# A two-branch mixer layer on one core: the first branch gated and split per head pair, the first attention group's preparation recorded beside the last scan

## The chip, the cores and the metric

One Trainium2 chip, one of its cores. The metric is device time in microseconds for one execution of the whole program, as the median of several runs. The engines are TensorE (PE, its weight loads PEld), VectorE (DVE), ScalarE (ACT), GpSimd (POOL) and SyncE (SP, which here only issues DMA transfers).

## The reference

One layer of a hybrid model over 640 tokens (128 of context, 512 latent), width 1024:

```
h = rmsnorm(x) * (1 + scale) + shift                     # scale, shift, gate from the condition
za, ga, q, kb, vb, gb, ma, mb = split(h @ w_in)          # one wide projection
r, k, v, wd, ad = split(short_conv(za))
for d in (forward, backward):                            # RWKV-7 scan, 16 heads of 64
    s = s * w_t + (s @ -kk_t) (kk_t a_t) + v_t k_t ;  y_d = s @ r_t
y = groupnorm(y_fwd + y_bwd) * ln_w + ln_b + bonus
branch_a = (y * silu(ga)) @ w_oA
o = banded grouped-query attention(rope(q), rope(kb), vb) + cached context keys, with a sink
branch_b = (o * silu(gb)) @ w_oB
out = x + gate * ((sigmoid(ma) * branch_a + sigmoid(mb) * branch_b) @ w_out) ; rmsnorm
```

The outputs are the two normed token blocks, the context's new keys and values, and the final scan states.

## The kernel before

**Layout.** Channels lie on the 128 partitions, the 640 tokens along the free axis. Each large product is in float32r with split operands: x = hi + lo, w = hi + lo, and three matmuls (hi·hi, hi·lo, lo·hi) per 128-row block. One block of 128 output columns is 48 matmuls of 128x320 in two PSUM halves (tag `g`, two buffers). Weights are loaded raw (`wr`, three buffers of 256 KB), cast on ACT (`wh`) and subtracted on POOL (`wl`).

**First stage: scan and filler.** The 16 heads are eight pairs (`NPAIR`), pair 0 to pair 7. For each pair there are `front` (decays, keys), `back` and `invert` (the inverse of the chunk matrices), `items` (five sets of chunk products), `chain` (ten dependent steps of the scan: two over the context, eight over the latents) and `finish` (group norm, transposes to `yT`, the bonus `bv` added on POOL, store to `a_dram[i]`). The matmuls that don't depend on the scan, the projections of the pairs and the *filler* (44 blocks: `kb`, `vb`, `q`, `ga`, `gb`, `ma`, `mb`, each spilled to DRAM), fill PE between the steps. `deal` writes out this order: a model clock (`Clock`) advances with each recorded instruction, and after every six filler matmuls each stream (`chains`, `finishes`, `all_items`, `fronts`, `backs`, in that order of right of way) is stepped where its model time has come. PE, ACT, DVE and POOL execute this part in the recorded order. Each engine runs its instructions strictly in order; an instruction that waits holds up those behind it.

**Between the stages.** `gate_rows` (16 products with `wg`, 256 KB each, through the `wr` buffers) and all that follows are placed by the scheduler by priority: earlier code first, `tc.cur_priority` moves it. So some of it lands among the last instructions of the scan.

**Second stage: attention and branch A.** `v_side` transposes cached keys and values, `k_side(g)` and `q_side(g)` rotate (`rope`) and split keys and queries of group g (0 to 3), `attend(g)` computes the softmax and the products with the values. The first call of the generator `branch_a` loads the eight `a_dram[k]` as `lda`, gates them with `ga` and splits them into `ah` and `al` (DVE, ACT, DVE); each further call is one of its eight blocks of 48 matmuls. The list `NBA` says how many blocks stand behind each group, `GPREP` behind which group the preparation is recorded.

**Third stage.** `branch_b` (8 blocks of 48) and `output` (240 matmuls, final norm).

Names in the profile: `g<-hh,wh` is a filler matmul, `g<-wg` a gate row, `st<-U,XT`, `st<-SB`, `ur<-SB,S`, `st<-SB,S`, `ur<-St,ar` are the five groups of matmuls of a chain step, `mi<-ident 32x320` is the second stage of `invert`, `g<-ah` is branch A, `ur<-KH,qt` a score product, `nm` a row maximum, `den` the softmax's denominator. All instructions recorded through `Timed` have the line of that helper (L139).

Of the kernel before, what the change touches and what calls it, by code (L numbers as in the profile page):

```python
# [51 lines left out]
GPREP = 1  # L52
PPREP = -600
NBA = [0, 3, 3, 2]
# [116 lines left out]
def hybrid_step(ctx, tc, a):  # L171
# [323 lines left out]
    def spill(col, dst, kind):  # L495

        def ev(half, o, s):
            t = T([P, HALF], "stg", 2, name="stg")
            if kind == "plain":
                act.copy(out=t, in_=o)  # L500
            else:
                act.activation(out=t, in_=o, func=AF.Tanh, scale=0.5)

            def rest():
                if kind == "silu":
                    dve.scalar_tensor_tensor(out=t, in0=t, scalar=1.0, in1=o, op0=ALU.add, op1=ALU.mult)
                nc.sync.dma_start(out=dst[:, s], in_=t)
            return rest
        return gemm_block(w_in, col, hh, hl, ev)
# [26 lines left out]
    def filler():  # L536

        for nm, col, nb, kind in (("kb", COL_KB, 2, "plain"), ("vb", COL_VB, 2, "plain"), ("q", COL_Q, 8, "plain"),
                                  ("ga", COL_GA, 8, "silu"),
                                  ("gb", COL_GB, 8, "silu"), ("ma", COL_MA, 8, "tanh"), ("mb", COL_MB, 8, "tanh")):  # L540
            for b in range(nb):
                spills[nm, b] = dram_.tile([P, TOK], F32, name="sp_%s%d" % (nm, b))
                yield spill(col + P * b, spills[nm, b], kind)
# [35 lines left out]
    a_dram = [dram_.tile([P, TOK], F32, name=f"a_dram{i}") for i in range(8)]  # L579
# [588 lines left out]
    def rope(x, outs):  # L1168

        sh = T([P, LAT], "tmp", 3, name="sh")  # L1170
        dve.stream_shuffle(out=sh, in_=x, mask=[(p + 16) % 32 for p in range(32)])
        t1 = T([P, LAT], "tmp", 3, name="t1")
        pool_e.tensor_tensor(out=t1, in0=x, in1=cosT, op=ALU.mult)
        dve.tensor_tensor(out=sh, in0=sh, in1=sinT, op=ALU.mult)
        for rows, dst in outs:
            dve.tensor_tensor(out=dst, in0=t1[rows], in1=sh[rows], op=ALU.add)

    def v_side():
        ck = T([P, 4, CH], "S", 5, name="ck")
# [4 lines left out]
        pt = PSC()  # L1184
        for b in range(2):
            pe.transpose(out=pt[:, b * P:(b + 1) * P], in_=ck[:, 2 * b:2 * b + 2, :].rearrange("p g d -> p (g d)"),
                         identity=ident)
        act.copy(out=kp.rearrange("p b x -> p (b x)"), in_=pt[:, 0:2 * P])
        vt_ = [T([P, 256], "SB", 10, name="vtok") for _ in range(5)]
        for b in range(2):  # L1190
            vz = unspill("vb", b, "rkv", 3)
            for t0, nt in ((0, 4), (4, 1)):
                pt = PSC()
                for t in range(nt):
                    pe.transpose(out=pt[:, t * P:(t + 1) * P], in_=vz[:, (t0 + t) * P:(t0 + t + 1) * P], identity=ident)
                for t in range(nt):
                    act.copy(out=vt_[t0 + t][:, P * b:P * b + P], in_=pt[:, t * P:(t + 1) * P])
# [6 lines left out]
    def k_side(g, kp):  # L1204
# [9 lines left out]
        pt = PSC()  # L1214
        pe.transpose(out=pt[:, 0:CH], in_=R[0:64, 6 * P:], identity=ident[0:64, 0:64])
        if g % 2 == 0:
            kt.append(T([P, 2, CH], "lraw", 1, name="kt"))
        act.copy(out=kt[-1][:, g % 2, :], in_=pt[:, 0:CH])
        if g % 2:
            nc.sync.dma_start(out=a["new_k"][0, 0, g - 1:g + 1].rearrange("g t d -> t g d"), in_=kt[-1])  # L1220
        rope(R[:, P:P + LAT], [(slice(0, P), R[:, P:P + LAT])])
# [4 lines left out]
        act.copy(out=H, in_=R)  # L1226
        pool_e.tensor_tensor(out=L, in0=R, in1=H.bitcast(F32), op=ALU.subtract)
# [4 lines left out]
    def q_side(g):  # L1232

        Q = []
        for b in range(2):
            q = unspill("q", 2 * g + b, "rkv", 3)
            rope(q[:, CTX:TOK], [(slice(0, P), q[:, CTX:TOK])])
# [8 lines left out]
            for h in range(2):  # L1246
                hr, lr = slice(64 * h, 64 * h + 64), slice(64 - 64 * h, 128 - 64 * h)
                act.copy(out=qs[h][hr, :], in_=q[hr, :])
                dve.tensor_tensor(out=qs[h][lr, :], in0=q[hr, :], in1=qs[h][hr, :].bitcast(F32),
# [285 lines left out]

    with tc.tile_pool(name="psc", bufs=1, space=PSUM) as pools["scan"], tc.manual_schedule(engines=ORDERED):
        deal(products(plan()), [chains(), finishes(), all_items(), fronts(), backs()])
# [3 lines left out]
    cosT = T([P, LAT], "kk", 1, name="cosT")  # L1541
    sinT = T([P, LAT], "cs", 1, name="sinT")
    nc.scalar.dma_start(out=cosT, in_=a["c_cos"])
    nc.scalar.dma_start(out=sinT, in_=a["c_sin"])
# [10 lines left out]
    kp, vt_, cv = v_side()  # L1555
    ba = branch_a()
    nxt = k_side(0, kp), q_side(0)
    for g in range(4):
        (KH, KL), Q = nxt
        if g < 3:  # L1560
            nxt = k_side(g + 1, kp), q_side(g + 1)
# [66 lines left out]
```

## Time and profile before

| | us |
|---|---|
| median of 3 runs (range) | 1475.28 (1470.62 to 1478.62) |
| the profiled execution, its span | 1471.97, 1470.2 |
| PE busy, share of the span | 1307.1, 89% |
| DVE, ACT, POOL busy | 791.8, 677.0, 455.1 |
| mean granted TensorE clock | 0.941 |

Where times below are points, they are microseconds from the span's start. A clock of 1.00 is 2.4 GHz, 0.50 is 1.2 GHz.

### The profile page before, as it was taken

The numbers are of one execution on the slowest core, as the hardware profiler recorded it, in microseconds if no ns is written. First come the engines' busy times: TensorE is split into PE (matmuls) and PEld (weight loads), VectorE is DVE, ScalarE is ACT, GpSimd is POOL, SyncE is SP. The second block draws the span as 40 slices with busy tenths as digits, with TensorE's granted clock in tenths as the row PEclk, the third lists the DMA queues.
The fourth block names the chain that finished last, engine by engine and source line by source line (L and its number), as shares of the span: only waits on it lengthen the run. The fifth ranks groups of instructions, "written<-read, shape, count | busy, mean of one in ns | idle before, by whom it ended". The sixth has DMA issues, their size and how long they took to land.

```text
span 1470.2 us, 40278 instructions
## 1 busy us (share of the span) xinstructions
PE 1307.1 (89%) x16959; PEld 1079.7 (73%) x16959; DVE 791.8 (54%) x1818; ACT 677.0 (46%) x1661; POOL 455.1 (31%) x476
## 2 busy tenths in 40 slices
PE   5699999999989999998998999999852889999996
PEld 0499888888878878887887878887441456668975
DVE  2446724654663455475464246336218887763547
ACT  2435563464365346436534635633524456554222
POOL 0333343343233234333332323331214031324530
PEclk9699999999999999999999999999955699999999
DMA  9143322222221222222231231322412341225532
GB/s 324 40 125 116 122 63 82 83 68 85 87 75 58 88 65 89 82 80 82 82 92 57 80 93 57 91 88 85 128 54 82 103 125 50 87 69 179 164 108 94
DMA packets 154419, 139.05 MB, mean 95 GB/s; under 512 B 16435, under 2 KB 130294, under 8 KB 154238
## 3 DMA queue, kind: packets, MB, share of 16 engines
q1 hardware_dynamic: 144328, 126.27, 27.8%
q10 hardware_dynamic: 9910, 10.21, 2.1%
q8 instruction: 133, 2.18, 0.6%
q14 instruction: 48, 0.39, 0.1%
HBM read 102.88 MB, written 33.56 MB: 93 GB/s over the span
## 4 chain that ended last, share of the span: by engine, by line
PE 64%; DVE 12%; issue 7%; ACT 6%; DMA 4%; POOL 2%; SPq 0%; DVEq 0%; ACTq 0%; POOLq 0%
PE g L139 34%; PE mi L139 10%; PE st L139 8%; PE sc L139 7%; PE ur L139 5%; DMA wr<-in_w_oB 1%; DMA wo<-in_w_out 1%; POOL wl L139 1%; DVE St L139 1%; DVE ytok L139 1%; DVE X L139 1%; ACT SB L139 1%; DVE o L139 1%; POOL wol L139 1%; ACT L139 1%
## 5 line engine op out<-in xcount | busy, mean ns | idle before, releaser
L139 POOL TENSOR_TENSOR wl<-wr,wh 128x512 fp32r<-128x512 f32 x170 | 229.4, 1352 | 666.8 <-ACT wh L139 620.0
L139 PE MATMUL g<-hh,wh 128*128 128x320 f32 (+1 forms) x1104 | 376.4, 341 | 11.4 <-DVE stg L139 4.6
L139 PE MATMUL g<-hl,wh 128*128 128x320 f32 (+1 forms) x1104 | 346.6, 314 | 1.7 <-POOL hl L139 1.5
L139 PE MATMUL g<-hh,wl 128*128 128x320 f32 (+1 forms) x1104 | 346.4, 314 | 0.0
L139 PEld LDWEIGHTS g<-hh,wh 128*128 128x128 f32 x1104 | 211.4, 191 | 31.0 <-issue 6.5
L139 PEld LDWEIGHTS g<-hl,wh 128*128 128x128 f32 x1104 | 211.9, 192 | 3.2 <-POOL hl L139 2.5
L139 PEld LDWEIGHTS g<-hh,wl 128*128 128x128 f32 x1104 | 212.4, 192 | 2.4 <-issue 1.9
L139 ACT CAST wh<-wr 128x512 fp32r<-128x512 f32 x170 | 104.4, 619 | 15.5 <-DMA wr<-in_w_oB 7.8
L139 ACT COPY SB<-st 64x128 f32<-64x128 f32 x160 | 41.6, 260 | 146.1 <-PE st L139 145.2
L139 DVE SCALAR_TENSOR_TENSOR St<-St,pc,st 128x64 f32<-128x64 f32 x128 | 30.2, 277 | 121.8 <-PE st L139 98.8
L139 ACT COPY U<-st 128x128 f32<-128x128 f32 x80 | 21.2, 266 | 159.0 <-DVE St L139 141.2
L139 DVE SCALAR_TENSOR_TENSOR stg<-g,vt,stg 128x127 f32<-128x127 f32 (+1 forms) x144 | 60.8, 436 | 62.0 <-ACT stg L139 59.4
L139 PE MATMUL mi<-ar,bk 64*64 64x64 f32 (+1 forms) x960 | 71.8, 248 | 7.5 <-DVE XT L139 7.4
L139 DVE TENSOR_TENSOR U<-ur,U 128x128 f32<-128x128 f32 x72 | 20.8, 289 | 94.7 <-PE ur L139 79.7
L139 POOL TENSOR_TENSOR S<-S,smask 128x512 f32<-128x512 f32 x40 | 50.3, 1256 | 63.5 <-ACT S L139 63.5
L139 ACT COPY SB<-sc 64x256 f32<-64x256 f32 (+1 forms) x160 | 55.2, 372 | 31.2 <-PE sc L139 29.4
L139 PEld LDWEIGHTS mi<-ar,bk 64*64 64x64 f32 (+1 forms) x960 | 61.7, 157 | 9.2 <-issue 6.8
L139 DVE TENSOR_TENSOR S<-sc,smask 128x512 f32<-128x512 f32 x40 | 27.4, 685 | 61.4 <-PE mi L139 46.0
L139 ACT ACTIVATE Pl<-ur,nm 128x384 f32<-128x384 f32 (+1 forms) x64 | 40.6, 635 | 36.9 <-DVE nm L139 30.1
L139 PE MATMUL ur<-KH,qt 128*128 128x512 f32 (+2 forms) x80 | 35.1, 443 | 22.7 <-ACT Pc L139 10.1
L139 ACT COPY PT<-sc 128x512 f32<-128x512 f32 x60 | 35.1, 584 | 39.3 <-PE sc L139 37.7
L139 DVE TENSOR_REDUCE nm<-ur 128x1 f32<-128x384 f32 (+2 forms) x68 | 41.5, 623 | 19.5 <-PE ur L139 18.7
(284 smaller groups left out, 2916.5 us busy)
## 6 DMA issues: line engine op xcount, KB each, us to landing
wr<-in_w_in SPq DMA_DIRECT2D x138, 256.0 KB
sp_rkv<-stg SPq DMA_DIRECT2D x48, 160.0 KB
rkv<-sp_rkv SPq DMA_DIRECT2D x24, 320.0 KB
wa_t<-in_w_ada SPq DMA_DIRECT2D x11, 512.0 KB
wg<-in_w_ada SPq DMA_DIRECT2D x16, 256.0 KB
wr<-in_w_oA SPq DMA_DIRECT2D x16, 256.0 KB
wr<-in_w_oB SPq DMA_DIRECT2D x16, 256.0 KB
wo<-in_w_out SPq DMA_DIRECT2D x16, 256.0 KB
```

The lines of the kernel that those rows point to most:

```text
L139: return f(**kw)
```

## The change

1. `finish` does the gating: when the pair's block of `ga` has been spilled, it loads it, multiplies, splits into hi and lo, and stores both halves, so `a_dram[i]` is [128, 2, 640]. The filler begins with `ga` so that it is there. `branch_a`'s first call is now 16 loads straight into `ah` and `al`, and is recorded ahead of group 0 instead of behind group 1; `NBA` goes from [0, 3, 3, 2] to [2, 3, 2, 1].
2. `finishes` moves behind `chains`, `all_items`, `fronts` and `backs`.
3. `v_side`, `k_side(0)`, `q_side(0)` become generators and are dealt with the last scan as three more streams, last in right of way; groups 1 to 3 run them through at once (`whole`) as before. They use other buffers; the five value tiles become one, evacuated with one instruction per PSUM tile.

```diff
-GPREP = 1
 PPREP = -600
-NBA = [0, 3, 3, 2]
+NBA = [2, 3, 2, 1]
...
-        for nm, col, nb, kind in (("kb", COL_KB, 2, "plain"), ("vb", COL_VB, 2, "plain"), ("q", COL_Q, 8, "plain"),
-                                  ("ga", COL_GA, 8, "silu"),
-                                  ("gb", COL_GB, 8, "silu"), ("ma", COL_MA, 8, "tanh"), ("mb", COL_MB, 8, "tanh")):
+        for nm, col, nb, kind in (("ga", COL_GA, 8, "silu"), ("kb", COL_KB, 2, "plain"), ("vb", COL_VB, 2, "plain"),
+                                  ("q", COL_Q, 8, "plain"), ("gb", COL_GB, 8, "silu"), ("ma", COL_MA, 8, "tanh"), ("mb", COL_MB, 8, "tanh")):
...
         pool_e.tensor_tensor(out=yT, in0=yT, in1=bv, op=ALU.add)
-        nc.sync.dma_start(out=a_dram[i], in_=yT)
-        yield
+        yield lambda: done.get(("ga", i))
+        sg = T([P, TOK], "bv", 1, name="us_ga")
+        nc.sync.dma_start(out=sg, in_=spills["ga", i])
+        clock.run.ready = max(clock.run.ready, clock.at["pe"] + 5)
+        yield
+        dve.scalar_tensor_tensor(out=yT, in0=yT, scalar=0.5, in1=sg, op0=ALU.mult, op1=ALU.mult)
+        yield
+        hi = T([P, TOK], "bv", 1, F32R, name="ah")
+        act.copy(out=hi, in_=yT)
+        nc.sync.dma_start(out=a_dram[i][:, 0], in_=hi.bitcast(F32))
+        yield
+        dve.tensor_tensor(out=yT.bitcast(F32R), in0=yT, in1=hi.bitcast(F32), op=ALU.subtract)
+        nc.sync.dma_start(out=a_dram[i][:, 1], in_=yT)
+        yield
...
         for k in range(KB):
-            f = T([P, TOK], ("tmp", "ytok")[k % 2], 1, name="lda")
-            nc.sync.dma_start(out=f, in_=a_dram[k])
-            sg = unspill("ga", k, "rkv", 1)
-            dve.scalar_tensor_tensor(out=f, in0=f, scalar=0.5, in1=sg, op0=ALU.mult, op1=ALU.mult)
             hi = T([P, TOK], "h", 16, F32R, name="ah")
             lo = T([P, TOK], "h", 16, F32R, name="al")
-            act.copy(out=hi, in_=f)
-            dve.tensor_tensor(out=lo, in0=f, in1=hi.bitcast(F32), op=ALU.subtract)
+            nc.sync.dma_start(out=hi.bitcast(F32), in_=a_dram[k][:, 0])
+            nc.sync.dma_start(out=lo.bitcast(F32), in_=a_dram[k][:, 1])
...
+    def first_values():
+        last = us[NPAIR - 1]
+        yield lambda: last.get("itemized") and last.get("prepared")
+        first["v"] = yield from v_side()
+
+    def first_keys():
+        last = us[NPAIR - 1]
+        yield lambda: "q" in first and "kp" in first and last.get("prepared")
+        first["k"] = yield from k_side(0, first["kp"], ("DG", "E"))
+
+    def first_queries():
+        yield lambda: us[NPAIR - 1].get("ready") and us[NPAIR - 2].get("finished") and us[NPAIR - 1].get("itemized")
+        for tag, src in (("kk", "c_cos"), ("cs", "c_sin")):
+            trig.append(T([P, LAT], tag, 1, name=src))
+            nc.scalar.dma_start(out=trig[-1], in_=a[src])
+        first["q"] = None
+        first["q"] = yield from q_side(0, ("ytok", "rkv"))
...
-        deal(products(plan()), [chains(), finishes(), all_items(), fronts(), backs()])
+        deal(products(plan()), [chains(), all_items(), fronts(), backs(), finishes(), first_values(), first_queries(), first_keys()])
...
+    base = tc.cur_priority
+    tc.cur_priority = PPREP + base
+    next(ba, None)
+    tc.cur_priority = base
...
-        if g == GPREP:
-            tc.cur_priority = PPREP + base
-            next(ba, None)
-            tc.cur_priority = 2000000 + base
```

What the order of instructions becomes, at three places.

**PE at the end of the filler.** Before, the last filler matmuls are followed by the last two of pair 6's ten chain steps:

```order
L139 MATMUL g<-hh,wl 128x320
L139 MATMUL g<-hl,wh 128x320
L139 MATMUL st<-U,XT 64x64 x4
L139 MATMUL g<-wg,csil 2x512
L139 MATMUL st<-SB 64x64 x4
```

Now the last of pair 6's steps starts 42 filler matmuls ahead of this place, and pair 7's `invert` follows at once:

```order
L138 MATMUL g<-hh,wl 128x320
L138 MATMUL g<-hl,wh 128x320
L138 MATMUL mi<-ident 32x320 x4
L138 MATMUL mi<-X,DG 32x32 x40
L138 MATMUL mi<-ident 32x320 x4
```

The two steps moved ahead of the filler's end; of the 16 `wg` products three instead of seven stand between the filler's end and pair 7's first step.

**PE in pair 7's chain, from its sixth step on.** Before, the steps stand alone:

```order
L139 MATMUL ur<-St_375,ar 64x64 x8
L139 MATMUL st<-U,XT 64x64 x4
L139 MATMUL st<-SB 64x64 x4
L139 MATMUL ur<-SB,S 64x64 x4
L139 MATMUL st<-SB,S 64x64 x4
```

Now branch A's products with the first seven pairs (42 matmuls) and the values' transposes (`vz`) stand between the parts of three steps; the first of them are ahead of the sixth step's start:

```order
L138 MATMUL sc<-ident,ck 128x128 x2
L138 MATMUL g<-ah,wh 128x320
L138 MATMUL g<-ah,wl 128x320
L138 MATMUL g<-al,wh 128x320
L138 MATMUL g<-ah,wh 128x320
L138 MATMUL g<-ah,wl 128x320
L138 MATMUL ur<-St_375,ar 64x64 x8
L138 MATMUL sc<-ident,vz 128x128 x4
L138 MATMUL g<-al,wh 128x320
L138 MATMUL st<-U,XT 64x64 x4
```

**DVE ahead of the first softmax's denominator** (pair 7's norm ends with `ytok<-ytok,gny`). Before, 28 rows stand between the two, with the keys and queries of groups 0 and 1; these are the last of them:

```order
L139 TENSOR_REDUCE nm<-ur 128x4
L139 TENSOR_TENSOR qt<-us_q,qt 64x640 x2
L139 TENSOR_TENSOR us_q<-t_14889,sh 128x512
L139 SCALAR_TENSOR_TENSOR nm<-nm,nsink 128x4
L139 TENSOR_REDUCE nm<-ur 128x1
L139 TENSOR_TENSOR den<-nm,sink 128x4
L139 STREAM_SHUFFLE sh<-R 128x512
L139 TENSOR_TENSOR qt<-us_q,qt 64x640 x2
L139 TENSOR_SCALAR nm<-nm,nsink 128x1
L139 TENSOR_TENSOR sh<-sh,sinT 128x512
L139 TENSOR_TENSOR den<-den,ssum 128x4
```

Now it is these, with pair 7's gating and split among them; group 0's keys and queries, and the first maxima, stand ahead of the norm's end:

```order
L138 TENSOR_TENSOR ytok<-ytok,gny 128x640
L138 STREAM_SHUFFLE sh<-R 128x512
L138 TENSOR_TENSOR sh<-sh,c_sin 128x512
L138 TENSOR_TENSOR R<-t_14940,sh 128x512
L138 STREAM_SHUFFLE sh<-us_q 128x512
L138 TENSOR_TENSOR sh<-sh,c_sin 128x512
L138 TENSOR_TENSOR us_q<-t_14954,sh 128x512
L138 STREAM_SHUFFLE sh<-us_q 128x512
L138 SCALAR_TENSOR_TENSOR yT<-yT,us_ga 128x640
L138 TENSOR_TENSOR qt<-us_q,qt 64x640 x2
L138 TENSOR_TENSOR yT<-yT,ah 128x640
L138 TENSOR_TENSOR den<-den,ssum 128x4
```

One `sh<-sh,c_sin` stands between the last two. The denominator moved from behind two groups' preparation to behind one group's.

## Rows read from the trace of the kernel before

**Rows 1.** Windows by stage: length; busy PE, PEld, DVE, ACT, POOL; clock; DMA share, GB/s

```profile
900.00:1013.00 113.00, 108.97 (x1826) 94.54 (x1825) 53.61 (x126) 53.18 (x143) 35.12 (x43) 0.98 0.27 82
1013.00:1044.40 31.40, 26.08 (x875) 17.25 (x873) 11.78 (x34) 15.00 (x42) 6.17 (x9) 0.89 0.33 99
1044.40:1102.50 58.10, 38.75 (x556) 26.75 (x554) 12.26 (x41) 18.30 (x61) 10.67 (x13) 0.70 0.28 84
1102.50:1141.80 39.30, 10.45 (x33) 6.61 (x33) 35.39 (x65) 16.70 (x42) 16.65 (x10) 0.50 0.26 78
1141.80:1200.00 58.20, 48.59 (x247) 29.97 (x247) 51.07 (x118) 32.87 (x81) 9.66 (x7) 0.82 0.39 117
1200.00:1342.70 142.70, 134.09 (x864) 96.32 (x863) 95.43 (x264) 75.88 (x194) 35.74 (x25) 0.98 0.26 81
1342.70:1470.20 127.50, 113.50 (x648) 102.20 (x648) 70.79 (x172) 35.05 (x74) 45.13 (x32) 0.97 0.44 138
```

**Rows 2.** Timeline of DVE from pair 7's norm to the first denominator

```profile
1103.16 0.82 DVE L139 TENSOR_REDUCE mu<-ytok 128x10 f32<-128x640 f32 x1
...
1110.74 0.82 DVE L139 TENSOR_TENSOR ytok<-ytok,gny 128x640 f32<-128x640 f32 x1
...
1119.39 3.50 DVE L139 TENSOR_TENSOR qt<-us_q,qt 64x640 fp32r<-64x640 f32 x2
...
1133.84 0.68 DVE L139 TENSOR_REDUCE nm<-ur 128x4 f32<-128x512 f32 x1
...
1141.83 0.15 DVE L139 TENSOR_TENSOR den<-den,ssum 128x4 f32<-128x4 f32 x1
```

**Rows 3.** Groups on DVE, 1102 to 1470: busy, mean ns

```profile
L139 DVE TENSOR_TENSOR qt<-us_q,qt 64x640 fp32r<-64x640 f32 x16 | 16.3, 1020 | 0.5
...
L139 DVE TENSOR_TENSOR al<-lda,ah 128x640 fp32r<-128x640 f32 x8 | 6.5, 818 | 0.0
...
L139 DVE SCALAR_TENSOR_TENSOR lda<-lda,us_ga 128x640 f32<-128x640 f32 x8 | 6.4, 821 | 0.1
```

**Rows 4.** Tile `ah`: ns least/median/most, first and last start

```profile
L139 ACT CAST ah<-lda x8: 714/724/732, 1162.8 to 1189.2; 128x640 fp32r<-128x640 f32 x8
```

**Rows 5.** Pieces of the chain that ended last, 950 to 1300: start, us

```profile
1063.84 3.76 DMA wr<-in_w_oA
...
1247.33 2.52 DMA us_ma<-sp_ma
```

**Rows 6.** SP's own waits, 300 to 1000: total us, times, longest

```profile
SPq L402 <- POOL wl L139: 193.4, 62, 11.4
```

**Rows 7.** Timeline of PE around the filler's end and pair 7's chain: start, length

```profile
1009.42 0.46 PE L139 MATMUL ur<-St,ar 64*64 64x64 f32 x16
...
1011.92 0.31 PE L139 MATMUL g<-hl,wh 128*128 128x320 f32 x1
...
1022.86 0.81 PE L139 MATMUL mi<-ident 32*32 32x320 f32 x8
...
1044.45 0.45 PE L139 MATMUL st<-SB,S 64*64 64x64 f32 x8
...
1093.26 0.70 PE L139 MATMUL ur<-St,ar 64*64 64x64 f32 x16 [1.54 <-DVE ytok L139]
...
1098.72 0.70 PE L139 MATMUL ur<-St,ar 64*64 64x64 f32 x16 [1.22 <-DVE ytok L139]
...
1101.73 0.64 PE L139 MATMUL ur<-SB,S 128*64 128x64 f32 x8
```

**Rows 8.** Timeline of PE in branch A: eleven spacings between these two

```profile
1336.01 0.31 PE L139 MATMUL g<-al,wh 128*128 128x320 f32 x1
...
1337.62 0.31 PE L139 MATMUL g<-ah,wl 128*128 128x320 f32 x1
```

**Rows 9.** Tile `bv`, the same columns

```profile
L139 POOL TENSOR_TENSOR yT<-yT,bv x8: 1537/1546/1573, 312.7 to 1114.0; 128x640 f32<-128x640 f32 x8
```

**Rows 10.** Window 1046 to 1050, the columns of rows 1

```profile
1046.00:1050.00 4.00, 4.00 (x54) 2.31 (x52) 0.71 (x2) 1.07 (x5) 0.00 (x0) 1.00 0.76 234
```

More of the change, by code (lines that the diff above doesn't have):

```diff
@@ L493, in conv_block, with spill @@
         return gemm_block(w_in, c0, hh, hl, ev, 2)
-    def spill(col, dst, kind):
+    done = {}
+    def spill(col, dst, kind, key):
         def ev(half, o, s):
@@ L507, in rest @@
                 nc.sync.dma_start(out=dst[:, s], in_=t)
+                done[key] = half
             return rest
@@ L578, in hybrid_step @@
     pool_e.memset(ap_of(keep[:, 0:1], [(CH, NCH)]), 0.0)
-    a_dram = [dram_.tile([P, TOK], F32, name=f"a_dram{i}") for i in range(8)]
+    a_dram = [dram_.tile([P, 2, TOK], F32, name=f"a_dram{i}") for i in range(8)]
     def project(i):
@@ L1183, in v_side @@
         kp = T([P, 2, P], "sub", 1, name="kp")
-        pt = PSC()
+        vz = T([P, 2, TOK], "bk", 3, name="vz")
+        for b in range(2):
+            nc.sync.dma_start(out=vz[:, b], in_=spills["vb", b])
+        clock.run.ready = clock.at["pe"] + 5
+        yield
+        pt = yield from take("sc")
         for b in range(2):
@@ L1187, in v_side @@
                          identity=ident)
+        yield
         act.copy(out=kp.rearrange("p b x -> p (b x)"), in_=pt[:, 0:2 * P])
-        vt_ = [T([P, 256], "SB", 10, name="vtok") for _ in range(5)]
+        give("sc")
+        first["kp"] = kp
+        yield SOON
+        vt = T([P, 5, 256], "bk", 3, name="vtok")
+        vt_ = [vt[:, t] for t in range(5)]
         for b in range(2):
-            vz = unspill("vb", b, "rkv", 3)
             for t0, nt in ((0, 4), (4, 1)):
-                pt = PSC()
+                pt = yield from take("sc")
                 for t in range(nt):
-                    pe.transpose(out=pt[:, t * P:(t + 1) * P], in_=vz[:, (t0 + t) * P:(t0 + t + 1) * P], identity=ident)
-                for t in range(nt):
-                    act.copy(out=vt_[t0 + t][:, P * b:P * b + P], in_=pt[:, t * P:(t + 1) * P])
+                    pe.transpose(out=pt[:, t * P:(t + 1) * P], in_=vz[:, b, (t0 + t) * P:(t0 + t + 1) * P],
+                                 identity=ident)
+                yield
+                act.copy(out=vt[:, t0:t0 + nt, P * b:P * b + P], in_=pt[:, :nt * P].rearrange("p (t x) -> p t x", x=P))
+                give("sc")
+                yield SOON
         nc.sync.dma_start(out=a["new_v"][0, 0].rearrange("g t d -> t g d"),
@@ L1213, in k_side @@
             act.copy(out=ap_of(R[hr, 0:1], [(5 * P, 2), (1, P)]), in_=bcast(kp[rows, g // 2, :], 1, 2))
-        pt = PSC()
+        clock.run.ready = max(clock.run.ready, clock.at["pe"] + 5)
+        yield
+        pt = yield from take("sc")
         pe.transpose(out=pt[:, 0:CH], in_=R[0:64, 6 * P:], identity=ident[0:64, 0:64])
+        yield
         if g % 2 == 0:
@@ L1218, in k_side @@
         act.copy(out=kt[-1][:, g % 2, :], in_=pt[:, 0:CH])
+        give("sc")
         if g % 2:
             nc.sync.dma_start(out=a["new_k"][0, 0, g - 1:g + 1].rearrange("g t d -> t g d"), in_=kt[-1])
-        rope(R[:, P:P + LAT], [(slice(0, P), R[:, P:P + LAT])])
+        yield from rope(R[:, P:P + LAT], tags)
         if g % 2:
@@ L1230, in hybrid_step, with q_side @@
     alt = [0]
-    def q_side(g):
+    def q_side(g, tags=("tmp", "tmp")):
         Q = []
+        loaded = [unspill("q", 2 * g + b, "rkv", 3) for b in range(2)]
+        clock.run.ready = clock.at["pe"] + 5
+        yield
         for b in range(2):
-            q = unspill("q", 2 * g + b, "rkv", 3)
-            rope(q[:, CTX:TOK], [(slice(0, P), q[:, CTX:TOK])])
+            q = loaded[b]
+            yield from rope(q[:, CTX:TOK], tags)
             if g < 3:
@@ L1534, in deal, with whole @@
                 clock.at["pe"] += 0.1
+    def first_values():
[13 more added lines that the diff above has]
+        first["q"] = yield from q_side(0, ("ytok", "rkv"))
+    def whole(steps):
+        clock.run = Run(steps, clock)
+        while True:
+            try:
+                next(steps)
+            except StopIteration as e:
+                clock.run = None
+                return e.value
     with tc.tile_pool(name="psc", bufs=1, space=PSUM) as pools["scan"], tc.manual_schedule(engines=ORDERED):
-        deal(products(plan()), [chains(), finishes(), all_items(), fronts(), backs()])
+        deal(products(plan()), [chains(), all_items(), fronts(), backs(), finishes(), first_values(), first_queries(), first_keys()])
     for _ in gate_rows():
@@ L1554, in hybrid_step @@
     dve.tensor_scalar(out=nsink, in0=sink, scalar1=-1.0, scalar2=None, op0=ALU.mult)
-    kp, vt_, cv = v_side()
+    kp, vt_, cv = first["v"]
     ba = branch_a()
-    nxt = k_side(0, kp), q_side(0)
+    nxt = first["k"], first["q"]
+    base = tc.cur_priority
+    tc.cur_priority = PPREP + base
+    next(ba, None)
+    tc.cur_priority = base
     for g in range(4):
@@ L1560, in hybrid_step @@
         if g < 3:
-            nxt = k_side(g + 1, kp), q_side(g + 1)
+            nxt = whole(k_side(g + 1, kp)), whole(q_side(g + 1))
         attend(g, Q, KH, KL, vt_, cv)
```

28 lines of the change are left out of this document (14 added, 14 removed).

## The prediction

> **What bounds the kernel now.** I read the windows by stage first, then PE's timeline where the table shows PE idle, then DVE's there. Until 1013 PE is busy for 108.97 of 113.00 us at clock 0.98 [rows 1]: the filler bounds it, and what DVE, ACT and POOL do beside it is hidden as long as PE need not wait for it. Then come three stretches in which it doesn't. From 1013.0 to 1044.4 pair 7's inverse runs with the rest of pair 6; from 1044.4 to 1102.5 pair 7's chain runs nearly alone, PE busy for 38.75 of 58.10, the mean clock 0.70; from 1102.5 to 1141.8 PE has 10.45 us of work in 39.30, at 0.50, and DVE 35.39 [rows 1]. The reader is to see there that DVE is the bound in that stretch: its timeline starts with pair 7's norm at 1103.16, which ends at 1111.56, and then the queue holds keys and queries of two groups; the first row maximum comes at 1133.84, the denominator is closed at 1141.83 [rows 2]. From 1141.8 to 1200.0 DVE has 51.07 of 58.20 and PE 48.59 at clock 0.82, from 1200 to 1342.7 PE has 134.09 of 142.70: PE is the bound again, and stays it to the end but for the final norm [rows 1]. So the place to win is 1013 to 1200, 187 us, in which PE does far less than it could.
>
> **The change part by part.** The sum is made against the profiled execution, 1471.97 us, which is 3.3 us under the median of 1475.28.
>
> *Filler and finishes (pairs 0 to 6).* Each finish gains two DVE operations of 128x640, an ACT cast, one more load and one more store. DVE 0.82 + 0.82 us and ACT 0.72 [rows 3, 4], on engines that are busy for 53.6 and 53.2 of 113 us there [rows 1]: work alone costs nothing while PE is the bound. What may cost is the wait. The gating stands in DVE's queue behind a load that starts only when POOL's addition has released `bv`; behind it stand the chain's additions and the convolution's edges, which free PSUM for PE. A load of the same 320 KB takes 2.52 us [rows 5], and the model clock keeps the gating 5 us behind the load's issue, so DVE waits only where SP or POOL lag by more than 2.5 us. SP does lag: its weight loads waited 193.4 us in 62 waits for POOL, 3.1 each, the longest 11.4 [rows 6]. Bounds: 0, and 7 x 11.4 = 80. A wait must exceed the margin and then PE's own slack, so I take 0.4 us a pair, **+3**. The order of spills (`ga` first) changes no count. Moving `finishes` last costs nothing by itself, since chain i waits only for finish i-2.
>
> *Chain start.* Pair 7's first step follows `invert`: from 1022.86 to 1044.45, 21.6 us [rows 7]. Before, this stage stood 10.9 us behind the last filler matmul (1011.92), because two steps of pair 6 and gate rows came first. Now it follows at once, so 10.9 us go. The two steps' matmuls and some of pair 7's items move in front of the filler's end, where PE pays for them: five groups a step of about 0.46 us at full clock [rows 7], 4.6 for two. **-6** (bounds -11 and 0).
>
> *Chain length.* Ten steps in 58.1 us, of which PE is idle for 19.4 [rows 1]. Added on PE: 42 products of branch A at (1337.62 - 1336.01)/11 = 0.146 us [rows 8], 6.1 us, and four more gate rows; they fit into the idle time, but each group delays the step behind it a little. Added on DVE: group 0's two query blocks and its keys, 13 operations of 0.7 to 1.0 us, about 10 us where DVE had 12.26 of 58.10; on ACT casts and copies, about 7 where it had 18.30 [rows 1]. Four steps of five hand-overs each meet them: 20 hand-overs, a chance of about a third to find the engine taken, half an operation (0.4 us) to wait, some 3 us. And the first branch A products need weights: the load 3.76 us [rows 5], then ACT and POOL's split, while only one chain step (5.46 us at half clock, 1093.26 to 1098.72 [rows 7]) lies between the last gate row and them, and the sixth step stands behind them on PE: some 3 us more, and 2 for contention below. Against it the added work holds TensorE at full clock for longer: `ur<-St` takes 0.46 us at full and 0.70 at half clock [rows 7], about 1 us a step, three steps. Together **+5** (bounds -4 and +20).
>
> *DVE beside POOL.* Two `qt` subtractions took 3.50 us together at 1119.39 [rows 2], with POOL at work beside them, against 0.82 for a subtraction of the same width [rows 3]: 0.93 lost on each. The mean of `qt` is 1.02 [rows 3], 0.2 lost. Of the operations moved into the chain ten have two SBUF inputs: they lose 2 us by the mean, which is in the term above, and 9 by the pair at 1119.39, 7 more. The Trainium skill, *SBUF — State Buffer*, section "Who interferes with whom", has a rule that speaks against the change: a DVE instruction with two SBUF inputs and a GpSimd instruction that reads SBUF exclude each other for the whole instruction. By that rule, with 1.54 us for a POOL operation, all ten could be held, and the chain's sum would be 13 us larger than mine; the mean in the rows is far below that.
>
> *Start of attention.* From the norm's end (1111.56) to the closed denominator (1141.83) it took 30.3 us [rows 2]. Now group 0 is ready before, and what is left on DVE is one rotation each of keys and queries of group 1, and pair 7's gating, which sets the length: transposes and `yT` 2.4 us (POOL's addition began at 1114.0), the addition 1.54 [rows 9], the load 2.52 [rows 5], gating 0.82, two `qt` subtractions 2.0, cast and split 1.5, one more product 0.8 [rows 3, 4]: some 12. Two maxima now stand inside the norm, 1.6. 30.3 - 12 - 1.6 = 16.7, **-16** (bounds -18 and -8, if the load waits as long as SP's worst).
>
> *Attention with branch A.* From 1141.8 to 1342.7, 200.9 us, PE had 48.59 x 0.82 + 134.09 x 0.98 = 171 us of work in full-clock terms [rows 1]. 6.1 of it now lies in the chain, 165 is left. At the density of 1200 to 1342.7 (131.4 of 142.7, 0.92) that is 179 us, 21 less. Preparing branch A also leaves DVE, 8 x (0.82 + 0.82) = 13.1 us [rows 3] of the 51.07 in the stretch where DVE was the bound, and two blocks instead of none stand ready to fill group 0. But the last group keeps one block instead of two, 7 us less of cover for its softmax. I take **-16** (bounds -24 and -6). The eight 128x640 stores and loads more cost bandwidth where 82 to 117 GB/s are used and 234 were reached [rows 1, 10].
>
> *Sum:* 3 - 6 + 5 - 16 - 16 = -30. 1471.97 - 30 = 1442; on the median's footing 1445. I predict **1444**.
>
> **Rivals.** *The chain is stretched* (gain 5 to 20, about 1462). Twelve loads of `ah` and `al`, 3.93 MB, now stand between the third and the fourth gate row's load in SP's order, and all gate rows of the chain behind them. At 234 GB/s [rows 10] they take 17 us, inside the 21.6 of `invert`; at the stretch's mean of 99 [rows 1] 40 us, and the chain's first steps wait for gate rows for up to 18 us. If all ten operations beside POOL lose what the pair at 1119.39 lost, that is 7 us more. For it: PE takes these products in order. Against it: in the window of [rows 10] the same queue ran at 234. It decides from about 110 GB/s downward.
>
> *More than forecast* (gain 52 to 60, about 1419): clock and density are full from the chain's end on, and the hand-overs cost nothing: -11 - 4 - 18 - 24 = -57. For it: PE is loaded in each stretch. Against it: DVE was busy for 88% between 1141.8 and 1200, and keeps groups 1's to 3's rotation.
>
> *Slower* (about 1495): the finishes hold DVE in the filler. It cancels the gain where each of seven waits costs PE more than (30 + 3)/7 = 4.7 us; at 7.5 us of SP's lag each it is 7 x 7.5 = 53 - 33 = 20 slower. For it: waits up to 11.4 [rows 6]. Against it: the mean is 3.1, and the loads are placed with a margin of 5.
>
> *No change:* the start is won but the last group's softmax and the chain give it back: a chain at +20 and attention at -6 leave 3 - 6 + 20 - 16 - 6 = -5.
>
> **How the numbers follow.** The forecast (1424 to 1456) has 0.60, the stretched chain 0.17, more than forecast 0.12, no change 0.06, slower 0.05. The range of 1414 to 1465 leaves out the slower case, no change, the stretched chain's end and a little below. A measurement of this kernel can tell about 0.5% (7 us) from no change. Faster by more than that takes in the forecast, the larger gain and most of the stretched chain: 0.87; within it 0.07; slower 0.06.
>
> **What would show it.** Right: until the last `g<-hh` no new DVE wait for a load, and that matmul some 5 us later than 1012; pair 7's chain starting about 21 us behind it and lasting about 60, with `g<-ah` inside it and the clock above 0.70; the first closed denominator some 24 us behind the chain's end instead of 39; no DVE operation on `lda`; branch B starting near 1313 instead of 1342.7. Wrong: DVE waiting for `us_ga` during the filler; PE waiting for `wg` or `wl` inside the chain by more than 10 us; or a branch B that starts no earlier though the denominator does, because DVE remains the bound.

## The result, and the profile after

The changed kernel takes 1454.28 us in the median of four runs (1451.12 to 1457.81); the kernel before took 1476.95 beside it (four runs, 1470.62 to 1479.28). The ratio is 0.987, 95% interval 0.9831 to 0.9909 (the quotient of the two medians is 0.985): faster, by 22.7 us in the medians where 31 were forecast. The two profiled executions lie closer together, spans of 1470.2 and 1455.8, 14.4 apart, since that of before was 5.0 under its median (1471.97 against 1476.95) and that of after 3.5 over (1457.81 against 1454.28). Below, stages are read from profiles and totals from ratios.

Windows by stage of the changed kernel (columns of [rows 1]), cut where the prediction cut them: filler, inverse, pair 7's chain, start of attention, attention in two parts, branch B and output:

```profile
900.00:1017.40 117.40, 114.12 (x2027) 99.80 (x2026) 58.38 (x126) 55.01 (x145) 37.62 (x48) 1.00 0.31 95
1017.40:1043.70 26.30, 18.96 (x636) 13.57 (x634) 5.72 (x21) 13.26 (x37) 4.65 (x6) 0.81 0.49 168
1043.70:1105.80 62.10, 46.74 (x605) 30.50 (x601) 24.15 (x58) 24.87 (x73) 17.31 (x17) 0.86 0.53 156
1105.80:1128.60 22.80, 6.79 (x23) 4.76 (x23) 20.55 (x45) 8.07 (x21) 7.83 (x5) 0.50 0.22 62
1128.60:1200.00 71.40, 57.61 (x304) 36.21 (x304) 56.58 (x138) 37.24 (x93) 17.53 (x12) 0.83 0.24 72
1200.00:1325.40 125.40, 116.79 (x764) 82.23 (x760) 79.58 (x234) 70.77 (x180) 31.45 (x22) 0.99 0.26 80
1325.40:1455.80 130.40, 115.48 (x648) 104.78 (x648) 66.72 (x172) 31.78 (x68) 43.07 (x31) 0.96 0.40 129
```

PE's timeline at the edges of these stages:

```profile
1017.40 0.31 PE L138 MATMUL g<-hl,wh 128*128 128x320 f32 x1
...
1043.67 0.45 PE L138 MATMUL st<-SB,S 64*64 64x64 f32 x8
...
1071.21 0.39 PE L138 MATMUL g<-ah,wh 128*128 128x320 f32 x1
1077.46 0.64 PE L138 MATMUL g<-ah,wl 128*128 128x320 f32 x1 [5.86 <-POOL wl L138]
...
1105.14 0.64 PE L138 MATMUL ur<-SB,S 128*64 128x64 f32 x8
...
1325.37 0.64 PE L138 MATMUL g<-bt,wh 128*128 128x320 f32 x1 [5.29 <-DVE stg L138]
```

Against the rows of before: the last filler matmul moved from 1011.9 to 1017.4 and the chain's first step from 1044.45 to 1043.67 [rows 7]. The chain takes 62.1 us instead of 57.9, at a clock of 0.86 instead of 0.70. From its end to the first closed denominator it is 22.8 instead of 39.5 us [rows 2, 7], from there to branch B 196.8 instead of 200.9, and from there to the end 130.4 instead of 127.5 [rows 1]. That is -0.8 + 4.2 - 16.6 - 4.1 + 2.9 = -14.4.

Pair 7's norm and the first closed denominator, with pair 7's gating between them, in DVE's timeline:

```profile
1114.43 0.82 DVE L138 TENSOR_TENSOR ytok<-ytok,gny 128x640 f32<-128x640 f32 x1
...
1124.16 1.39 DVE L138 SCALAR_TENSOR_TENSOR yT<-yT,us_ga 128x640 f32<-128x640 f32 x1
...
1128.63 0.16 DVE L138 TENSOR_TENSOR den<-den,ssum 128x4 f32<-128x4 f32 x1
```

PE has one new long wait inside the chain, 5.86 us for `wl`. POOL's timeline says why:

```profile
1057.31 1.19 POOL L138 TENSOR_TENSOR ar<-ar,pc 128x256 f32<-128x256 f32 x2
1071.99 2.49 POOL L138 TENSOR_TENSOR t<-us_q,c_cos 128x512 f32<-128x512 f32 x2 [13.49 <-DMA c_cos<-in_c_cos]
1074.45 1.29 POOL L138 TENSOR_TENSOR t<-R,c_cos 128x512 f32<-128x512 f32 x1
1075.68 2.96 POOL L138 TENSOR_TENSOR wl<-wr,wh 128x512 fp32r<-128x512 f32 x2
```

The subtraction that makes `wl` stands behind three rotations, and these behind the load of the cosines, which ACT issued at 1067.53, 4.5 us earlier.

### The profile page after: what moved, and what is told of

It is laid out like the page before. It is cut to its first block, busy times and chain, and to the rows that moved or that the text cites. A ratio compares the mean times of both kernels' runs of the same rounds, so it can differ in the third digit from the quotient of the medians.

```text
span 1455.8 us, 40281 instructions
## 1 busy us (share of the span) xinstructions
PE 1301.2 (89%) x16959; PEld 1075.5 (74%) x16959; DVE 799.1 (55%) x1818; ACT 677.0 (47%) x1655; POOL 456.3 (31%) x476
## 4 chain that ended last, share of the span: by engine, by line
PE 69%; DVE 11%; issue 7%; ACT 5%; POOL 2%; DMA 1%; SPq 0%; DVEq 0%; ACTq 0%; POOLq 0%
PE g L138 39%; PE mi L138 11%; PE sc L138 7%; PE st L138 7%; PE ur L138 5%; DVE X L138 2%; DVE M L138 2%; ACT SB L138 1%; DVE Pl L138 1%; DVE St L138 1%; DVE o L138 1%; ACT L138 1%; DMA sp_rkv<-stg 1%; DVE stg L138 0%; DVE nm L138 0%
## 5 line engine op out<-in xcount | busy, mean ns | idle before, releaser
L138 DVE SCALAR_TENSOR_TENSOR St<-St,pc,st 128x64 f32<-128x64 f32 x128 | 30.2, 277 | 124.1 <-PE st L138 100.3
L138 ACT COPY U<-st 128x128 f32<-128x128 f32 x80 | 21.3, 266 | 136.4 <-DVE St L138 116.8
L138 DVE TENSOR_TENSOR S<-sc,smask 128x512 f32<-128x512 f32 x40 | 27.3, 683 | 45.8 <-PE mi L138 24.9
L138 PE MATMUL g<-bt,wh 128*128 128x320 f32 x192 | 46.7, 320 | 5.3 <-DVE stg L138 5.3
```

The source lines that it names most:

```text
L138: return f(**kw)
```

## Experiments

The first table has the totals (ratio to the kernel before, with its interval), the second the stages of the one profiled execution, in us, read off PE's and DVE's timelines as above. "Start" is the chain's first step counted from the last filler matmul, "to den" is from the end of pair 7's norm to the first closed denominator, "attention" from there to the first product of branch B, "rest" from there to the end.

| run | ratio | 95% interval |
|---|---|---|
| the change | 0.987 | 0.9831 to 0.9909 |
| before_finishes_last | 0.9853 | 0.9821 to 0.9885 |
| before_ga_and_last | 1.0065 | 1.004 to 1.009 |
| finishes_second | 1.0028 | 1.0002 to 1.0054 |
| gated_only | 0.9928 | 0.9902 to 0.9953 |
| dealt_only | 0.9888 | 0.986 to 0.9916 |
| ga_fourth | 0.9799 | 0.9766 to 0.9833 |
| trig_early | 0.985 | 0.9822 to 0.9878 |
| ga_fourth_trig | 0.9773 | 0.9743 to 0.9803 |
| blocks_0332 | 0.9873 | 0.9843 to 0.9904 |
| evac_first | 0.9921 | 0.9892 to 0.995 |
| evac_and_ytok | 0.983 | 0.98 to 0.9861 |
| all_four | 0.9729 | 0.9694 to 0.9765 |

| run | last g<-hh | start | chain | to den | attention | rest |
|---|---|---|---|---|---|---|
| before | 1011.9 | 32.5 | 57.9 | 30.3 | 200.9 | 127.5 |
| the change | 1017.4 | 26.3 | 62.1 | 13.4 | 196.8 | 130.4 |
| before_finishes_last | 1026.8 | 5.2 | 56.5 | 30.2 | 202.0 | 125.9 |
| before_ga_and_last | 1020.9 | 30.1 | 60.9 | 30.3 | 201.8 | 126.5 |
| finishes_second | 994.1 | 76.4 | 58.1 | 13.3 | 198.6 | 130.3 |
| gated_only | 1017.4 | 26.5 | 53.2 | 32.6 | 192.0 | 127.8 |
| dealt_only | 1019.2 | 5.2 | 62.9 | 8.9 | 209.3 | 130.3 |
| ga_fourth | 1033.6 | -3.4 | 59.6 | 13.4 | 194.8 | 130.3 |
| trig_early | 1015.7 | 26.4 | 53.7 | 13.4 | 194.9 | 130.2 |
| ga_fourth_trig | 1030.8 | -3.4 | 58.9 | 13.4 | 197.2 | 130.2 |
| blocks_0332 | 1012.8 | 24.3 | 61.3 | 13.3 | 196.4 | 130.5 |
| evac_first | 1016.5 | 24.4 | 60.5 | 13.3 | 198.1 | 128.1 |

The times of one kernel spread over some 10 us, and one execution is profiled: the last filler matmul of four kernels that have the same order up to it came at 1012.8 to 1017.4. A single stage's difference of a few us is therefore not read as an effect unless several kernels repeat it. The ratios of the experiments come from three sets of runs, each with its own of the kernel before; where medians say something else than ratios, both are given. The last two runs of the first table are not in the second, as branch B starts inside attention there.

### Which part of the change gives what

**finishes_second** and **before_finishes_last** test the line on which the prediction had put no price. The first undoes it in the changed kernel, the second does it alone in the kernel before:

```diff
-        deal(products(plan()), [chains(), finishes(), all_items(), fronts(), backs()])
+        deal(products(plan()), [chains(), all_items(), fronts(), backs(), finishes()])
```

> The changed kernel with the finishes in their old place, second in right of way. Theory (the place decides how far the scan gets beside the filler: 698 matmuls then lie between the last filler matmul and pair 7's first U product instead of 328): the chain starts 10 to 18 us later, in all about 1466. Rival (the prediction: moving the finishes costs and gives nothing by itself): within 3 us of 1454.

> The kernel before with one line changed: the finishes last in right of way. Theory (that place alone moves pair 7's inverse into the filler: 80 matmuls instead of 456 then lie between the last filler matmul and the chain's first U product): the chain starts some 5 us behind the last filler matmul instead of 32.5, in all 15 to 22 us faster than before, about 1453. Rival (the prediction: the place costs and gives nothing by itself): within 4 us of the kernel before, 1472.

Both went the theory's way, the first by more than it said: 1478.17 us where it gave about 1466. The changed kernel without that line is no faster than the kernel before (1.0028), and the kernel before with that line alone gains as much as the whole change. PE's timelines, with the last filler matmul and the chain's first step of finishes_second and then of before_finishes_last:

```profile
994.07 0.31 PE L138 MATMUL g<-hl,wh 128*128 128x320 f32 x1
...
1070.50 0.69 PE L138 MATMUL st<-SB,S 64*64 64x64 f32 x8
```

```profile
1026.84 0.31 PE L139 MATMUL g<-hl,wh 128*128 128x320 f32 x1
...
1032.06 0.45 PE L139 MATMUL st<-SB,S 64*64 64x64 f32 x8
```

Read the distance of the two rows: what the scan has left to do when the filler is used up runs with nothing beside it. It is 76.4 us with the finishes second and `ga` first, 5.2 with the finishes last and the old filler. It is not the gain itself: the more of the scan runs inside the filler, the later the filler ends. In before_finishes_last it ended at 1026.8 instead of 1011.9, so that the chain began 12.4 us earlier than in the kernel before, not 27.3.

**before_ga_and_last** puts `ga` first in the filler as well, still without gating or dealing; **ga_fourth** takes `ga` back to its old place in the changed kernel:

```diff
-        for nm, col, nb, kind in (("ga", ...), ("kb", ...), ("vb", ...), ("q", ...), ("gb", ...), ("ma", ...), ("mb", ...)):
+        for nm, col, nb, kind in (("kb", ...), ("vb", ...), ("q", ...), ("ga", ...), ("gb", ...), ("ma", ...), ("mb", ...)):
```

> The kernel before with two things changed: the finishes last, and the filler begins with ga. Theory (the two moves cancel each other: 438 matmuls lie in that gap again): the chain starts 28 to 34 us behind the last filler matmul, within 6 us of the kernel before. Rival (the order of the filler's blocks changes no count and so no time): as fast as the kernel before with the finishes last alone.

> The changed kernel with the filler's old order (kb, vb, q, then ga); the gating waits for its blocks. Theory (ga ahead of the plain blocks pushes pair 7's inverse behind the filler's end: 328 matmuls lie between the last filler matmul and the chain's first U product, 80 in the kernel without the gating): pair 7's chain now starts with the last filler matmul, some 20 us earlier by the clock, and everything behind it moves with it, less 3 to 6 us of a later filler end; in all about 1438 us. Rival (the gating's own work in the finishes is what costs at the filler's end, and held-back finishes make it worse): within 4 us of 1454 or slower.

The order of the filler's blocks does change the time. It turned a gain of 1.5% into a loss of 0.65% in the first, more than expected, and its removal brought the second to 0.9799. The gating did not need `ga` first: in ga_fourth a finish waits until its block is there. The last filler matmul and the chain's first step of before_ga_and_last:

```profile
1020.94 0.31 PE L139 MATMUL g<-hl,wh 128*128 128x320 f32 x1
...
1051.08 0.45 PE L139 MATMUL st<-SB,S 64*64 64x64 f32 x8
```

In ga_fourth PE starts the chain before the filler is done:

```profile
1030.18 0.45 PE L138 MATMUL st<-SB,S 64*64 64x64 f32 x8
...
1033.60 0.31 PE L138 MATMUL g<-hl,wh 128*128 128x320 f32 x1
```

The last product of pair 3's norm began at 691.6 in before_finishes_last and at 709.9 in before_ga_and_last, that of pair 2's at 568.7 and 571.8: the scan fell 15 us further behind there, in the middle of the filler, and by pair 6 it was 34.5 us behind (1010.6 and 1045.1). Why the written order comes out so is not measured; the model clock by which the streams are stepped charges a block of `ga` more work on VectorE than a plain one, which is a guess at the cause.

**gated_only** has the first group back behind the scan, **dealt_only** has the gating back in branch A (with the old filler order, the old block list and the old place of branch A's preparation).

> The changed kernel with the first group's values, keys and queries back behind the scan; gating, split and the 42 early products stay. Theory (the earlier start of attention is the dealing's; the chain's 5.9 us wait for wl is made by the dealt rotations that stand ahead of it on POOL): the wait for wl in the chain falls to under 2 us, the chain ends near 1098, and the first denominator closes 39 us behind it as before, near 1137; in all about 1463. Rival (the products' weights are late by themselves, from their load): the chain ends near 1105 all the same, the denominator closes near 1144, in all about 1470.

> The changed kernel with the gating and split back in the first call of the first branch (behind group 1), the blocks listed as [0, 3, 3, 2] and the filler's old order; only the first group's dealing and the place of the finishes remain. Theory (the gating saves nothing in attention, and its early products stretch pair 7's chain): the chain, without the 42 products, ends some 8 us earlier than the changed kernel's 1105, the first denominator closes near 1117, attention is as long as before (201 us), branch B starts near 1320, in all about 1451 us. Rival (the prediction's terms: the gating takes 16 us out of attention): attention is 213 us long, branch B starts near 1331, in all about 1460.

The first went by the theory in the chain (POOL is free, and the wait for `wl` is 0.91 us) and to 2 us in the total. Against before_ga_and_last it shows what the gating is worth: 1.0065 to 0.9928, by stages 3.5 in the filler's end, 3.6 in the start, 7.7 in the chain, 9.8 in attention, of which the two other stages take 3.6 back. The dealing on top of it, 0.9928 to 0.987, is not clear of the intervals. dealt_only fell between the two in the total, and its theory was wrong twice: attention is 209.3 us long, so the gating does save there, and the chain without the 42 products is 62.9 long, not shorter. What it gained came from a start 5.2 us behind the filler, which neither side had foreseen. (Its profiled execution, 1447.05, is the fastest of six with a median of 1456.05.) Against before_finishes_last, the dealing alone is worth nothing that the intervals show (0.9888 and 0.9853): 21.3 us less up to the denominator, 6.4 more in the chain, 7.3 more in attention, 4.4 more in the rest. The three kernels' windows over attention show where the work went (VectorE's busy time is the third figure behind the length):

```profile
1127.90:1329.90 202.00, 182.72 (x1108) 126.08 (x1108) 146.12 (x381) 109.04 (x275) 46.33 (x32) 0.93 0.30 91
```

```profile
1138.90:1330.90 192.00, 168.44 (x1060) 115.59 (x1060) 132.29 (x369) 105.34 (x271) 47.64 (x33) 0.94 0.24 74
```

```profile
1105.70:1315.00 209.30, 185.44 (x1108) 127.91 (x1109) 153.53 (x389) 114.49 (x285) 48.78 (x34) 0.90 0.29 89
```

They are before_finishes_last, gated_only and dealt_only. The gating takes 13.8 us of VectorE out of attention, and the dealing puts 7.4 in: group 1's preparation, which used to lie ahead of the first denominator. Attention's length followed, 10.0 less and 7.3 more. That points to VectorE's queue; no run changes its work alone.

### The wait in the chain

**trig_early** issues the two loads when pair 7's front is done; nothing else moves on any engine:

```diff
-        yield lambda: us[NPAIR - 1].get("ready") and us[NPAIR - 2].get("finished") and us[NPAIR - 1].get("itemized")
+        yield lambda: us[NPAIR - 1].get("ready")
         for tag, src in (("kk", "c_cos"), ("cs", "c_sin")):
...
+        yield lambda: us[NPAIR - 2].get("finished") and us[NPAIR - 1].get("itemized")
```

> The changed kernel with the two loads of cosines and sines issued when pair 7's front is done (some 100 us earlier); no other instruction moves on any engine. Theory (wl in the chain is late because POOL's queue stands still for the cosines until 1072): the 5.9 us wait for wl falls under 1.5, the clock stays at full in the sixth step, the chain ends 6 to 9 us earlier, in all about 1447. Rival (wl waits for the weights' own load and cast): the wait stays above 4 us, in all within 2 us of 1454.

> The same with the early cosines and sines as well. Theory: the two gains add, another 7 us, in all about 1431. Rival: with the chain's start at the filler's end other work hides the wait for wl, and the early load adds under 2 us.

The theory held. In trig_early POOL's rotations are done long before `wl` is wanted, and PE waits 0.47 us for it:

```profile
1059.30 1.28 POOL L138 TENSOR_TENSOR t<-R,c_cos 128x512 f32<-128x512 f32 x1
1067.52 1.27 POOL L138 TENSOR_TENSOR wl<-wr,wh 128x512 fp32r<-128x512 f32 x1 [6.94 <-ACT wh L138]
```

```profile
1068.85 0.41 PE L138 MATMUL g<-ah,wl 128*128 128x320 f32 x1 [0.47 <-POOL wl L138]
```

The chain is 53.7 us long, 8.4 less: 5.4 of the wait, and for the rest the clock, as far as the rows show (0.31 us for a product behind the wait instead of 0.47). The total agrees by the medians, 1447.08 against 1454.28; by the ratios, 0.985 and 0.987, it shows no gain beyond the intervals. With the filler's old order the early loads add little: ga_fourth waits 0.79 us by itself, and its median of 1442.8 differs by 3.4 from the 1439.4 with the early loads, inside the intervals.

### What sets the length of attention

**blocks_0332** has the old block list `[0, 3, 3, 2]`:

> The changed kernel with the old list of branch A's blocks, [0, 3, 3, 2]. Theory (the list hardly moves anything, since branch A has the lowest priority and fills gaps wherever it is written): within 3 us of 1454, attention as long as in the changed kernel. Rival (the prediction: two blocks behind group 0 fill its gaps, one block less behind the last group uncovers its softmax): attention's first 80 us or its end move by 5 us or more, one way or the other.

Nothing moved (attention 196.4 against 196.8). Branch A has the lowest priority, and where its blocks are written decides next to nothing.

**evac_first** gives the evacuation of branch A's blocks the highest priority; **evac_and_ytok** also loads all `us_ma` into the buffers `ytok`:

```diff
+                base = tc.cur_priority
+                tc.cur_priority = base - 2100000
                 dve.scalar_tensor_tensor(out=t, in0=tm[:, s], scalar=1.0, in1=o, op0=ALU.add, op1=ALU.mult)
+                tc.cur_priority = base
...
-            tm = unspill("ma", j, ("ytok", "rkv")[j % 2], 1)
+            tm = unspill("ma", j, "ytok", 1)
```

> The changed kernel with the evacuation of branch A's blocks on DVE ahead of all softmax work that is ready at the same time. Theory (in the first 25 us of attention TensorE has no filler, because the first block's two PSUM halves wait for DVE until 1156.5): the second block starts near 1140 instead of 1160.7, the first 80 us of attention lose 12 to 16 us to idling and the lower clock instead of 24, the 5.3 us wait ahead of branch B falls under 1.5; in all about 1443. Rival (the opening is bound by DVE's own softmax work): the second block may start earlier, but the opening is as long, and only the wait at the end goes; in all about 1450 to 1454.

> The run with the evacuations first, and beside it all eight us_ma loads into the ytok buffers. Theory (with the evacuations first TensorE ran out of work behind the last block of branch A, because that block's evacuation waited for us_ma behind us_gb in SP's queue, and branch B for the PSUM): branch B's products now stand among the last group's softmax, its first one some 15 to 25 us ahead of the last product with the values; in all 10 to 14 us faster than the run with the evacuations first alone, about 1446. Rival (attention's length is that of the softmax alone, and branch B needs its last groups anyway): branch B begins earlier but waits for them; within 4 us of 1456.

> The changed kernel with the four edits together: filler's old order, early cosines and sines, evacuations first, us_ma in ytok. Theory: what the run with the first two won, and 8 to 14 us of the attention's end on top: about 1428. Rival (the end of attention gives nothing): about 1439, as without the last two.

In evac_first my theory fell. Its first half came true: these are the first 80 us of attention, of the changed kernel and then of evac_first, the latter also with its last 22 us:

```profile
1128.60:1208.60 80.00, 64.96 (x343) 40.81 (x344) 64.39 (x160) 41.00 (x104) 18.84 (x13) 0.84 0.21 65
```

```profile
1124.20:1204.20 80.00, 71.75 (x458) 50.99 (x459) 68.73 (x179) 47.13 (x117) 23.63 (x17) 0.95 0.30 92
...
1300.00:1322.30 22.30, 11.96 (x44) 5.35 (x44) 5.62 (x14) 6.30 (x13) 5.95 (x4) 0.50 0.23 75
```

PE does 71.75 x 0.95 = 68 us of full-clock work instead of 64.96 x 0.84 = 55, and attention is not shorter (198.1 against 196.8). The total is no better either: 1458.21 us (0.9921) where the theory gave about 1443. Branch A runs out at 1290, and the last softmax goes on alone at half clock. Branch B might have filled that, but its first product waited. VectorE's and SP's timelines of evac_first show for what:

```profile
1320.13 1.75 DVE L138 SCALAR_TENSOR_TENSOR yb<-yb,us_gb 128x640 f32<-128x640 f32 x1 [3.01 <-DMA us_gb<-sp_gb]
1321.81 0.87 DVE L138 SCALAR_TENSOR_TENSOR stg<-us_ma,g 128x320 f32<-128x320 f32 x2
```

```profile
1317.15 0.33 SPq L548 DMA_DIRECT2D us_gb<-sp_gb  x1
1317.53 0.42 SPq L548 DMA_DIRECT2D us_ma<-sp_ma  x1
```

The last block's evacuation had its priority, but its `us_ma` was loaded only at 1317.5, behind the last group's `us_gb` in SP's queue; both PSUM buffers stayed taken until 1322. With the loads in `ytok`, branch B's first product starts 18.4 us ahead of the last product with the values:

```profile
1299.17 0.31 PE L138 MATMUL g<-bt,wh 128*128 128x320 f32 x1
...
1317.59 0.65 PE L138 MATMUL mi<-PT,cv 128*64 128x256 f32 x4 [0.73 <-ACT PT L138]
```

What that gave is not clear from the totals: by the ratios, 0.9921 to 0.983, some 13 us, as the theory asked; by the medians, 1458.21 to 1452.87, 5, with the time inside the rival's 4 us of 1456. The profiles speak for the rival. From the first denominator to the end it is 326.2 us in evac_first, 324.0 in evac_and_ytok and 327.2 in the changed kernel; to the last product with the values it is 190.6, 188.2 and 189.9. Neither the denser opening nor the full clock at the end shortened the softmax by more than 2 us, and branch B, begun earlier, ended hardly earlier. **all_four**, with the filler's old order, the early loads and these two, is the fastest version found: 1437.04 us, 0.9729 of the kernel before, near its rival's 1439 and not its theory's 1428. Its gain over ga_fourth_trig (0.9773) is inside the intervals.

## Why the prediction was right, and where not

The time lies inside the forecast, in part by luck. Of the five terms only the start of attention came as it was worked out. Two steps that were priced at nothing each moved the kernel by 10 to 31 us, in opposite directions, and most of the gain put on attention did not come.

**Filler and chain start** (+3 and -6; measured -0.8 together). The number is nearly right and the working wrong. That the last `g<-hh` would come about 5 us later was right (5.5), and so was that VectorE would not wait for `us_ga`: the trace of the changed kernel has no such wait. But "Moving `finishes` last costs nothing by itself" and "The order of spills (`ga` first) changes no count" are the two steps that failed. In the kernel before, the first is worth 22 us (0.9853), and the second on top of it costs 31 (0.9853 to 1.0065). In the changed kernel, undoing the first costs 23 (0.987 to 1.0028) and undoing the second gives 10 (0.987 to 0.9799). The 5.5 us fit was helped by the execution: with the same order the last filler matmul came 0.9 to 5.5 us later than before. I counted instructions and waits for each, where the question was how far the scan gets before the filler runs out. The written order showed the difference: in before_finishes_last 80 matmuls lie between the last filler matmul and the chain's first `st<-U,XT`, in the changed kernel 328.

**Chain length** (+5; measured +4.2). Right in size, with the terms mis-sized both ways. The higher clock from the added products was put at 3 us. gated_only has the 42 products and a chain of 53.2 us at a clock of 0.92 where before_ga_and_last, without them, has 60.9 at 0.72:

```profile
1043.90:1097.10 53.20, 42.56 (x594) 26.79 (x588) 13.19 (x42) 17.68 (x58) 11.18 (x13) 0.92 0.45 139
```

```profile
1051.10:1112.00 60.90, 39.43 (x560) 25.67 (x556) 12.11 (x41) 17.79 (x58) 10.67 (x13) 0.72 0.33 101
```

Against the two other chains without products and dealing (57.9 and 56.5) it is 3 to 5 us, net of what the products themselves delay; no run separates the two. The wait for branch A's weights was put at 3 us for load and split, and measured 5.9 for another reason, POOL's queue behind the cosines. The loads of `ah` and `al` ahead of the gate rows, the rival's mechanism, cost 0.8 us of waiting in all; DMA ran at 168 GB/s in the stretch of the inverse. By the prediction's figures (3.93 MB in 21.6 us) these loads begin to outlast `invert` below 182 GB/s; its 110 is where they would cost some 14 us.

**Start of attention** (-16; measured -16.6). Right, mostly by its own steps: 13.4 us from the norm's end to the denominator where 12 were worked out, and a norm 0.3 us longer where 1.6 were. POOL's addition (1117.67) and the load behind it (issued at 1119.23) came as foreseen. The gating began only at 1124.16, behind a VectorE operation that POOL had held; three operations met POOL there and lost 3.3 us, which the term had left out.

**Attention with branch A** (-16; measured -4.1). This is the term whose size was wrong and by which the total missed. PE's work did fall as worked out, but the length was taken from that work at a density of 0.92, and evac_first and evac_and_ytok show that denser work does not shorten it. By the runs, the gating gives 9.8 there and the dealing takes 4.8 back (7.3 without the gating). The changed kernel and its six variants in the table that keep gating and dealing lie between 194.8 and 198.6, so the size of the 4.8 is rough. The 13.1 us that leave VectorE were counted; group 1's preparation, which had just been taken off the start of attention, was not put back in. The price for the last group's cover, 7 us, was for nothing (blocks_0332).

**Branch B to the end** was left out; it is 2.9 us longer in the profile (4.4 in dealt_only against before_finishes_last). The time goes at its start: behind the wait of 5.29 us, which counts to attention, PE ran the first 4 us at a clock of 0.50, and did 363 products in the first 57.3 us where the kernel before did 383; 20 products at 0.146 us [rows 8] are 2.9 us. The changed kernel, then the kernel before:

```profile
1325.40:1382.70 57.30, 55.98 (x363) 55.72 (x364) 25.77 (x42) 15.54 (x32) 30.50 (x22) 0.95 0.54 165
```

```profile
1342.70:1400.00 57.30, 56.76 (x383) 56.09 (x384) 31.66 (x45) 20.39 (x40) 33.72 (x25) 1.00 0.62 187
```

In dealt_only, which starts this stage at full clock, PE waited 2.7 us for `bl` instead.

## What to carry to other kernels

Where work that depends on itself runs beside independent filler, first look at how much of it is left when the filler ends: a change of priority or of the filler's order that touches no count moved this by tens of us here. Work that is taken off one stretch has to be put back where it lands, and denser work beside a stretch need not shorten it. Undo each line of a change singly: here two lines worked against each other, and taking one of them back raised the gain from 1.3 to 2.0%.

## What the runs showed of the hardware

A VectorE operation of 128x512 or 64x640 with two SBUF inputs, begun while a GpSimd operation ran, was not slowed by a share, but ended some 0.6 us after the other's end. VectorE and POOL in the changed kernel:

```profile
1085.13 1.94 DVE L138 TENSOR_TENSOR qt<-us_q,qt 64x640 fp32r<-64x640 f32 x1
...
1120.94 2.55 DVE L138 TENSOR_TENSOR us_q<-t,sh 128x512 f32<-128x512 f32 x1 [1.19 <-POOL t L138]
```

```profile
1083.87 2.52 POOL L138 TENSOR_TENSOR wl<-wr,wh 128x512 fp32r<-128x512 f32 x2 [5.23 <-ACT wh L138]
...
1120.84 2.10 POOL L138 TENSOR_TENSOR KL<-R,KH 128x896 fp32r<-128x896 f32 x1
```

The first ends at 1087.07, POOL's at 1086.39; the second at 1123.49, POOL's at 1122.94; alone they take 0.82 and 0.69. Seven more of 128x512 and 128x640 between 1074 and 1325 ended 0.55 to 0.68 after POOL's. This agrees with the rule in the Trainium skill, *SBUF — State Buffer*, section "Who interferes with whom", that the two exclude each other for the whole instruction. In the chain only two operations were held so (the other took 1.80 instead of 0.69 at 1074.49), so it cost 2.2 us there: the prediction's 2, reached by a mean, and not the 9 of its upper case.

In pair 7's inverse PE stood still for 7.2 us in three waits (2.27, 3.42 and 1.54) for which the trace names no releaser; in the thirteen other executions such waits there come to 0.9 to 8.4. What it waits for stays open.
